# A two-layer hybrid backbone on one core: rows of the Gram tile cleared once per wave on VectorE, rounded row maxima, and a rotation that keeps its own tile

## The chip, the core and the metric

The kernel runs on one core of a Trainium2 chip. The core has five engines that each work through their own list of instructions in a fixed order: TensorE (PE; its weight loads, PEld, are listed apart), VectorE (DVE), ScalarE (ACT), GpSimd (POOL) and SyncE (SP, which here only issues transfers). They wait for each other through semaphores alone. The metric is the time of one execution in microseconds of device time (us), the median of several runs.

## What is computed

Two layers over 256 context tokens and 1024 latent tokens of width 1024. Each layer has one input projection whose columns feed three groups of heads (a bidirectional RWKV-7 recurrence, grouped-query attention with a 2-D rotary rotation, and neighbourhood attention), then one output projection and a layer norm. The parts that the change touches:

```python
def _rwkv7_step(S, inp):                       # 6 heads, both directions, token by token
    r, w, k, v, kk, b = inp
    sa = jnp.einsum('bhvk,bhk->bhv', S, kk)
    S = S * w[:, :, None, :] - sa[..., None] * b[:, :, None, :] + v[..., None] * k[:, :, None, :]
    return S, jnp.einsum('bhvk,bhk->bhv', S, r)

def _apply_axial_rope(x, cos, sin):            # on the latent tokens of q and k of the grouped-query heads
    x1, x2, x3, x4 = jnp.split(x, 4, axis=-1)
    rotated = jnp.concatenate([-x2, x1, -x4, x3], axis=-1)
    return (x * cos[:, None] + rotated * sin[:, None]).astype(x.dtype)

    def one_block(qi):                         # both attentions: a softmax over scores
        s = jnp.einsum('bqgrd,bsgd->bgrqs', qi, keys).astype(jnp.float32)
        p = jax.nn.softmax(s, axis=-1).astype(vals.dtype)
        return jnp.einsum('bgrqs,bsgd->bqgrd', p, vals)
```

## The kernel before

The order of instructions on each engine is set by a scheduler when the program is built; the source order and the dependences are its input. So a small edit can shift the places of many instructions.

**The input projection** (`layer_proj`) multiplies 29 column blocks of 128 with the modulated stream, each product split in three passes of rounded parts (lines 203 to 205, tile `pj`). `qk_proj` handles the keys and the three pairs of query heads of grouped-query attention. It evacuates into `raw` (tile `qr`, two buffers, line 348), normalises it in place, fetches the rotated halves into `rot` by four transfers (line 364), multiplies `rot` by the sine and `raw` by the cosine on POOL (lines 365, 366), adds on DVE into `raw` (line 367) and stores `raw` to DRAM (line 368). The next but one `qk_proj` writes the same buffer of `raw`.

**The recurrence** (`rwkv`) runs in waves of 128 tokens, ten per layer, each with both directions and all six heads; a wave has four chunks of 32 tokens. `wave_pre`, `wave_gram`, `wave_low`, `wave_inv`, `wave_kt` and `wave_merge` prepare a wave two or three waves ahead. `wave_gram` leaves in `G` (six buffers) the masked products of the chunk's vectors. `wave_merge` multiplies blocks of `G` and of the inverse (tile `mg`, line 684): a first round whose result DVE masks into `di` (line 687), and a second round from which DVE makes `tt` (line 689). `wave_chain` then takes the four chunks one after the other: with a tile `X` that stacks, for each direction and head of a pair, the state (64 rows), the values `v` (32 rows, loaded from DRAM at line 706) and the solved rows `sa` (32 rows), it computes `rs` from `G` and `X` (line 713), `sa` from `tt` (line 724, copied into `X` at line 730), the next state `z` (line 734), which DVE scales into the next `X` (line 739), and the output `py` (line 754, in `out_step`, one chunk late). `X` has three buffers. The product for `rs` contracts over all 128 rows, the `sa` rows of the buffer among them, and these still hold what an earlier chunk left there. So POOL sets them to zero in each chunk (line 708, four instructions). The rows of the stacked tile that belong to `sa` are named by `QSA`, those of `v` by `QV`.

**Attention** (`attention`) runs two interleaved generators, woven by the scheduler with the recurrence. `pair_max` computes scores `sm` (line 894) and their row maxima on DVE (lines 896 to 901, tile `nm`, float32). A product with the identity turns each column of 128 maxima into a row, in float32 in the array's column group that begins at 64 (line 907, tile `mt`), and ACT copies it with rounding into row 64 of `q2` (line 908). `pair_main` computes the transposed scores `st` with that row as a 65th term (lines 963, 964), exponentiates (line 970) and multiplies with the values (line 948). Operands of type `F32R` are float32 rounded for a single pass in the array; a float32 product is issued as two instructions.

## Time and profile before

| what | value |
|---|---|
| median of 3 runs | 2448.75 us (2443.36 to 2449.61) |
| the profiled execution, its own time | 2449.5 us |
| its span, first to last instruction | 2447.7 us |
| mean granted TensorE clock | 0.934 of full speed |
| PE busy | 2206.0 us (90% of the span) |
| DVE busy | 1615.7 us (66%) |
| POOL busy | 1180.5 us (48%) |
| ACT busy | 1005.5 us (41%) |
| L907, the products that turn the maxima | 360 instructions, 52.8 us |
| L708, the zeroing of X's rows | 320 instructions, 81.7 us |

A row `L907 PE MATMUL mt<-c_ident,nm` reads: line 907, engine, operation, tile written, tiles read. Busy time of PE counts each product from its start to its modelled end, so overlapping products are counted once and a product's own duration is longer than its distance from the next. "Idle before" and "waits" name the instruction that the profile takes as the one that ended an engine's wait; for a wait on several semaphores it names one of them.

### The profile page before, as it was taken

The page shows a single profiled execution, that of the slowest core. Times are in us where ns is not written, and L with a number is a line of the kernel's source. Part 1 is how long each engine was busy: PE and PEld are TensorE (multiplying, and loading weights), DVE is VectorE, ACT ScalarE, POOL GpSimd, SP SyncE. Part 2 cuts the span into 40 slices and gives each one's busy share as a digit, 9 for nine tenths or more (in the row PEclk, how much of TensorE's full clock was granted, in tenths as well). Part 3 has the DMA queues.
Part 4 walks back from the last instruction along what each step waited for, and adds up shares of the span by engine and source line. Part 5 has one row for each costly group of instructions (what it writes and reads, how often), then busy time and mean ns, then how long its engine had stood idle before and what let it go on. Part 6 is the DMA issues. An engine that isn't in the chain of part 4 may idle for free. (4 is left out here: it accounts for less than half of the span.)

```text
span 2447.7 us, 57800 instructions
## 1 busy us (share of the span) xinstructions
PE 2206.0 (90%) x22616; PEld 1657.5 (68%) x22616; DVE 1615.7 (66%) x3063; ACT 1005.5 (41%) x2186; POOL 1180.5 (48%) x1438
## 2 busy tenths in 40 slices
PE   6999999997887898989999999899969888889897
PEld 3777898775555555555798777697746555556497
DVE  5687434445766878686387797524557788788746
ACT  3333413334544544454343443313345555545522
POOL 3465425424555555454155465533455565565453
PEclk9999999996887999989899999999968999999999
DMA  7344424527445544452233445335464545333342
GB/s 282 111 156 157 134 85 103 144 79 164 111 115 118 122 102 124 125 168 64 73 94 106 136 162 181 112 90 127 113 152 113 117 116 124 81 84 87 100 153 87
DMA packets 448241, 298.17 MB, mean 122 GB/s; under 512 B 249600, under 2 KB 395880, under 8 KB 446944
## 3 DMA queue, kind: packets, MB, share of 16 engines
q1 hardware_dynamic: 439936, 281.71, 41.9%
q0 software_dynamic: 7392, 10.28, 1.6%
q8 instruction: 178, 2.92, 0.5%
q10 hardware_dynamic: 640, 2.49, 0.4%
q14 instruction: 95, 0.78, 0.1%
HBM read 198.37 MB, written 91.79 MB: 119 GB/s over the span
## 5 line engine op out<-in xcount | busy, mean ns | idle before, releaser
L204 PE MATMUL pj<-hlo,wh 128*128 128x512 f32 (+1 forms) x1072 | 402.8, 376 | 13.1 <-DVE hlo L480 7.6
L203 PE MATMUL pj<-hhi,wh 128*128 128x512 f32 (+1 forms) x1072 | 403.2, 378 | 9.2 <-ACT qr L348 5.1
L205 PE MATMUL pj<-hhi,wl 128*128 128x512 f32 (+1 forms) x1072 | 402.0, 376 | 0.2 <-POOL wl L169 0.2
L204 PEld LDWEIGHTS pj<-hlo,wh 128*128 128x128 f32 x1072 | 205.7, 192 | 55.6 <-DVE hlo L480 7.7
L203 PEld LDWEIGHTS pj<-hhi,wh 128*128 128x128 f32 x1072 | 204.8, 192 | 54.3 <-issue 6.8
L169 POOL TENSOR_TENSOR wl<-wf,wh 128x512 fp32r<-128x512 f32 x104 | 142.9, 1379 | 202.7 <-ACT wh L168 185.4
L205 PEld LDWEIGHTS pj<-hhi,wl 128*128 128x128 f32 x1072 | 205.9, 192 | 38.6 <-issue 3.6
L896 DVE TENSOR_REDUCE mx<-sm 128x1 f32<-128x512 f32 (+1 forms) x372 | 199.1, 553 | 46.0 <-PE sm L894 43.7
L948 PE MATMUL y<-pt,v 128*64 128x256 f32 (+1 forms) x1392 | 214.0, 405 | 3.3 <-ACT pt L973 2.4
L970 ACT ACTIVATE pt<-st 128x512 f32<-128x512 f32 (+1 forms) x292 | 163.6, 583 | 129.5 <-PE st L964 125.7
L894 PE MATMUL sm<-k,q 128*128 128x256 f32 (+2 forms) x436 | 167.1, 429 | 34.6 <-DVE mx L896 26.8
L963 PE MATMUL st<-q,k 128*128 128x512 f32 (+3 forms) x376 | 165.9, 445 | 12.5 <-issue 3.5
L1197 PE MATMUL pj<-yl,wh 128*128 128x256 f32 x576 | 165.0, 289 | 2.0 <-POOL yl L1170 2.0
L1196 PE MATMUL pj<-yh,wh 128*128 128x256 f32 x576 | 162.8, 291 | 4.0 <-ACT wh L1147 2.1
L1198 PE MATMUL pj<-yh,wl 128*128 128x256 f32 x576 | 163.2, 288 | 0.1
L977 POOL TENSOR_TENSOR acc<-acc,pt 128x512 f32<-128x512 f32 x80 | 105.4, 1317 | 115.3 <-ACT pt L970 114.4
L948 PEld LDWEIGHTS y<-pt,v 128*64 128x64 f32 x1392 | 94.4, 144 | 90.8 <-issue 60.0
L894 PEld LDWEIGHTS sm<-k,q 128*128 128x128 f32 x436 | 82.8, 208 | 104.6 <-DVE mx L896 42.4
L964 PE MATMUL st<-q,k 65*128 65x512 f32 (+3 forms) x376 | 147.1, 395 | 0.6 <-ACT q L908 0.6
L625 DVE TENSOR_TENSOR G<-gt,msk 64x192 f32<-64x192 f32 (+1 forms) x320 | 110.5, 345 | 43.1 <-PE gt L620 32.0
L708 POOL MEMSET X<- 32x192 f32 x320 | 81.7, 255 | 89.1 <-PE py L754 59.9
L977 DVE TENSOR_TENSOR acc<-acc,pt 128x512 f32<-128x512 f32 x112 | 101.7, 918 | 30.3 <-ACT pt L970 29.8
(276 smaller groups left out, 5113.8 us busy)
## 6 DMA issues: line engine op xcount, KB each, us to landing
wf<-win SPq DMA_DIRECT2D x104, 256.0 KB
wm<-wmod SPq DMA_DIRECT2D x32, 512.0 KB
yf<-yg_d SPq DMA_DIRECT2D x72, 128.0 KB
wt<-wm SPq DMA_DIRECT2D x8, 1024.0 KB
gate_d<-o SPq DMA_DIRECT2D x32, 256.0 KB
wf<-wout SPq DMA_DIRECT2D x16, 512.0 KB
ldkk<-rw_d SPq DMA_DIRECT2D x40, 192.0 KB
ldkd<-rw_d SPq DMA_DIRECT2D x40, 192.0 KB
```

The lines of the kernel that those rows point to most:

```text
L203: nc.tensor.matmul(out=ps[:, :n], lhsT=wh, rhs=hhi[:, k, t0:t0 + n], start=(k == 0), stop=False)
L204: nc.tensor.matmul(out=ps[:, :n], lhsT=wh, rhs=hlo[:, k, t0:t0 + n], start=False, stop=False)
L205: nc.tensor.matmul(out=ps[:, :n], lhsT=wl, rhs=hhi[:, k, t0:t0 + n], start=False, stop=(k == KT - 1))
L894: nc.tensor.matmul(out=sp_[:, :o], lhsT=q[0][:, qc:qc + 128], rhs=k[0][:, c0:c0 + o], start=True, stop=True)
L896: nc.vector.tensor_reduce(out=mx[:, n_:n_ + 1], in_=sp_[:, :o], op=ALU.max, axis=AX.X)
L948: mm = nc.tensor.matmul(out=y[64 * i:64 * i + 64, a0:a1], lhsT=v[:, t, :], rhs=pt[:, p0:p0 + a1 - a0], start=start, stop=stop and at == le ...
L963: nc.tensor.matmul(out=o, lhsT=k[0][:, 128 * t:128 * t + 128], rhs=q[0][:, qa:qb], start=True, stop=False)
L970: nc.scalar.activation(out=pt[:, :w], in_=sp_[:, :w], func=AF.Exp)
L977: eng.tensor_tensor(out=acc[i][:, :w], in0=sums[i][:, :w], in1=pt[:, :w], op=ALU.add)
L1196: nc.tensor.matmul(out=p_, lhsT=wh[m][:, k], rhs=yh, start=(x_ == 0), stop=False)
L1197: nc.tensor.matmul(out=p_, lhsT=wh[m][:, k], rhs=yl, start=False, stop=False)
L1198: nc.tensor.matmul(out=p_, lhsT=wl[m][:, k], rhs=yh, start=False, stop=(x_ == KT - 1))
```

## The change

Three edits. First, in the recurrence, the zeroing of the `sa` rows of `X` in each chunk goes; in its place `wave_merge` sets the `sa` rows of columns 0 to 31 of `G` to zero on DVE, four instructions per wave, once the products of `mg` have read them. All three buffers of `X` are zeroed once at the start of a layer. Second, the maxima are kept rounded in a tile of 72 columns whose first 64 come from the identity; a weight of 65 columns that ends at the wanted one gives the row on partition 64 in one single-pass product over the whole array, with a rounded copy of the identity. Third, `qk_proj` adds into `rot` and stores from there, and the context columns of `raw`, which are not rotated, are stored by a transfer of their own right after the four that fetch the halves.

```diff
--- before.py
+++ after.py
@@ -362,10 +362,12 @@
             rot = sp.tile([128, TL], F32, tag="rot", name="rot")
             for q in range(4):
                 nc.sync.dma_start(out=rot[32 * q:32 * q + 32, :], in_=raw[32 * (q ^ 1):32 * (q ^ 1) + 32, TC:T])
+            if not lo:
+                nc.sync.dma_start(out=dst[:, :TC], in_=raw[:, :TC])
             nc.gpsimd.tensor_tensor(out=rot, in0=rot, in1=sin, op=ALU.mult)
             nc.gpsimd.tensor_tensor(out=raw[:, TC:], in0=raw[:, TC:], in1=cos, op=ALU.mult)
-            nc.vector.tensor_tensor(out=raw[:, TC:], in0=raw[:, TC:], in1=rot, op=ALU.add)
-            nc.sync.dma_start(out=dst[:, lo:], in_=raw[:, lo:])
+            nc.vector.tensor_tensor(out=rot, in0=raw[:, TC:], in1=rot, op=ALU.add)
+            nc.sync.dma_start(out=dst[:, TC:], in_=rot)
 
         def store(dst, b, o):
 
@@ -539,7 +541,8 @@
                 nc.vector.tensor_copy(g[o, :, :, p, :], ident[o, 64 * p:64 * p + 64].unsqueeze(1).unsqueeze(1).to_broadcast([64, 4, 3, 64]))
         NX = 3
         X = [rp.tile([128, 2, 3, 2, 64], F32, tag=f"X{i}", name=f"X{i}") for i in range(NX)]
-        nc.gpsimd.memset(X[0], 0.0)
+        for x in X:
+            nc.gpsimd.memset(x, 0.0)
         lin = rp.tile([128, 16, 16], F32, tag="lin", name="lin")
         nc.gpsimd.memset(lin, 0.0)
 
@@ -687,6 +690,11 @@
                     nc.vector.tensor_tensor(out=po, in0=mg, in1=omk.unsqueeze(1).unsqueeze(1).to_broadcast([128, 4, 3, 32]), op=ALU.mult)
                 else:
                     nc.vector.tensor_tensor(out=tt, in0=mg, in1=di[:, 1], op=ALU.subtract)
+
+            for d in range(2):
+                for p in range(2):
+                    q = QSA[d][p]
+                    nc.vector.memset(gs[d][q:q + 32, :, :, p, 0:32], 0.0)
             prep[w]["tt"] = tt
 
         def wave_chain(w):
@@ -702,10 +710,9 @@
                 for d in range(2):
                     t0 = 128 * wave_block(w, d) + 32 * jc[d]
                     for p in range(2):
-                        q, qs = QV[d][p], QSA[d][p]
+                        q = QV[d][p]
                         nc.sync.dma_start(out=x[q:q + 32, d, :, p, :],
                                           in_=vt_d[t0:t0 + 32, :].rearrange("t (c e v) -> t c e v", c=3, e=2)[:, :, p, :])
-                        ms = nc.gpsimd.memset(x[qs:qs + 32, d, :, p, :], 0.0)
                 for c in range(3):
                     for d in range(2):
                         for p in range(2):
@@ -738,7 +745,7 @@
                         o = slice(64 * p, 64 * p + 64)
                         up = nc.vector.tensor_tensor(out=xn[o, :, :, p, :], in0=z[o], in1=dcj(dc[o, 0, j], j), op=ALU.mult)
                     if j == 1:
-                        mark.update(v=up, g=ms)
+                        mark.update(v=up)
                 if yst is not None:
                     pend.append(lambda j=j, x=x, jc=jc: out_step(w, j, x, jc, gs, yst))
             for f in pend:
@@ -839,6 +846,14 @@
         py = es.enter_context(tc.tile_pool(name=f"py{l}", bufs=1, space=PSUM, side="right"))
         wn = es.enter_context(tc.tile_pool(name=f"wn{l}", bufs=1, **kw))
         ms = mod_spread(((1, 2),) if last else ((0, 2), (1, 1), (1, 0)), wn, pst)
+        identr = ap1.tile([128, 128], F32R, tag="identr", name="identr")
+        nc.vector.tensor_copy(identr, ident)
+
+        nms = [ap1.tile([128, 72], F32R, tag=f"nm{i}", name="nm") for i in range(2)]
+        for z in nms:
+            nc.vector.tensor_copy(z[:, 0:64], ident[:, 0:64])
+            nc.vector.tensor_copy(z[:, 64:72], ident[:, 0:8])
+        nj = [0]
         onec = ap1.tile([128, 32], F32, tag="onec", name="onec")
         nc.vector.memset(onec, 1.0)
 
@@ -882,7 +897,8 @@
 
         def pair_max(q, k, jobs, nq, bias):
 
-            nm = ap2.tile([128, 8], F32, tag="nm", name="nm")
+            nm = nms[nj[0] % 2]
+            nj[0] += 1
             for i, job in enumerate(jobs):
                 q0 = job["q0"]
                 for qt in range(nq // 128):
@@ -898,13 +914,13 @@
                             nc.vector.tensor_tensor_reduce(out=sp_[:, :o], in0=sp_[:, :o], in1=bias[0][:, bcol:bcol + o], scale=1.0, scalar=-3.0e38,
                                                            op0=ALU.add, op1=ALU.max, accum_out=mx[:, n_:n_ + 1])
                         if n_ == len(pcs) - 1:
-                            nc.vector.tensor_reduce(out=nm[:, 4 * i + qt:4 * i + qt + 1], in_=mx[:, :len(pcs)], op=ALU.max, axis=AX.X, negate=True)
+                            nc.vector.tensor_reduce(out=nm[:, 64 + 4 * i + qt:65 + 4 * i + qt], in_=mx[:, :len(pcs)], op=ALU.max, axis=AX.X, negate=True)
                         yield
             for i, job in enumerate(jobs):
                 q0 = job["q0"]
                 mt = pst.tile([128, 512], F32, tag="sm", name="mt", bufs=2)
                 for qt in range(nq // 128):
-                    nc.tensor.matmul(out=mt[64:65, 128 * qt:128 * qt + 128], lhsT=nm[:, 4 * i + qt:4 * i + qt + 1], rhs=ident, start=True, stop=True, tile_position=(0, 64))
+                    nc.tensor.matmul(out=mt[0:65, 128 * qt:128 * qt + 128], lhsT=nm[:, 4 * i + qt:4 * i + qt + 65], rhs=identr, start=True, stop=True)
                 nc.scalar.copy(q[1][64:65, q0:q0 + nq], mt[64:65, :nq])
                 yield
```

The order differs in many places; three are shown. The first is on DVE, where the merge of the fourth wave of the first layer stands, before (`acc`, `pt`, `mx`, `sm`, `nm`: attention; `yo`: the recurrence's output; `lin`, `nn`: the inverse of the next wave):

```order
L982 TENSOR_TENSOR acc_10158<-acc_10158,pt_10233 128x384
L687 TENSOR_TENSOR di<-mg,omk 128x384
L901 TENSOR_REDUCE nm<-mx 128x1
L972 TENSOR_TENSOR pt_10247<-st,bt 128x384
L972 TENSOR_TENSOR pt_10254<-st,bt 128x384
L792 TENSOR_REDUCE sm<-yo 128x6
L898 ISA sm,mx<-sm,bs 128x384
L898 ISA mx 128x1
L896 TENSOR_REDUCE mx<-sm 128x1
L645 COPY nn<-lin 64x256
L793 TENSOR_SCALAR sm<-sm 128x6
```

The same place on DVE after the change (line 690 is the former 687, line 912 the former 896, line 647 the former 644):

```order
L647 COPY nn<-lin 64x256
L998 TENSOR_TENSOR acc_10050<-acc_10050,pt_10124 128x384
L697 MEMSET G_2952 32x12x32 x2
L690 TENSOR_TENSOR di<-mg,omk 128x384
L697 MEMSET G_2953 32x12x32 x2
L988 TENSOR_TENSOR pt_10145<-st,bt 128x384
L917 TENSOR_REDUCE nm<-mx 128x1
L797 TENSOR_TENSOR yo<-yo,sm 128x384
L914 ISA sm,mx<-sm,bs 128x384
L914 ISA mx 128x1
```

Two of the four new instructions stand ahead of the mask that the second round of `mg` waits for, and two behind it, ahead of `tt`.

The second place is POOL, at the preparation of a later wave of the first layer (`G`, `lp`, `kb`: the wave's tiles; `acc`: attention's sums), before:

```order
L593 MEMSET G_2950 64x12x64 x2
L593 MEMSET G_2951 64x12x64
L708 MEMSET X_2967 32x3x64 x3
L593 MEMSET G_2951 64x12x64
L708 MEMSET X_2967 32x3x64
L570 DMA zs<-zs_d 98x128
L977 TENSOR_TENSOR acc_11072<-pt_11077,pt_11096 128x512
L570 DMA zs<-zs_d 98x128
L594 TENSOR_TENSOR G_2950<-ldkk,lp 64x3x4x32
L596 TENSOR_TENSOR G_2950<-ldr,lp 64x3x4x32
```

POOL after the change, at the same preparation (line 596 is the former 593):

```order
L596 MEMSET G_2954 64x12x64 x2
L596 MEMSET G_2955 64x12x64 x2
L998 TENSOR_TENSOR acc_10958<-acc_10958,pt_11063 128x384
L573 DMA zs<-zs_d 98x128
L998 TENSOR_TENSOR acc_10958<-acc_10958,pt_11081 128x256
L998 TENSOR_TENSOR acc_10959<-acc_10959,pt_11081 128x128
L890 TENSOR_TENSOR q_11282<-stg,q_11282 64x1280
L573 DMA zs<-zs_d 98x128
L1058 TENSOR_TENSOR ys<-ys,gtl 128x512
L597 TENSOR_TENSOR G_2954<-ldkk,lp 64x3x4x32
L599 TENSOR_TENSOR G_2954<-ldr,lp 64x3x4x32
```

What is gone are the zeroings of `X` between the others. No other engine takes over POOL's work; the four instructions per wave on DVE are all that is added there in the recurrence.

The third place is PE at the first wave of the first layer, where before the products for `rs` stood early, ahead of that wave's `mg` (line 684):

```order
L713 MATMUL ch<-X_2966,G_2949 32x64
L635 MATMUL kt<-c_ident,kb 128x128 x3
L713 MATMUL ch<-X_2966,G_2949 32x64
L713 MATMUL ch<-X_2966,G_2948 32x64 x2
L713 MATMUL ch<-X_2966,G_2949 32x64 x2
L713 MATMUL ch<-X_2966,G_2948 32x64 x2
L713 MATMUL ch<-X_2966,G_2949 32x64 x2
```

After the change they stand behind the `mg` products (line 687), which read what is then cleared:

```order
L720 MATMUL ch<-X_2970,G_2952 32x64
L203 MATMUL pj<-hhi,wh 128x512
L720 MATMUL ch<-X_2970,G_2952 32x64
L204 MATMUL pj<-hlo,wh 128x512
L687 MATMUL mg<-di 32x32 x48
L638 MATMUL kt<-c_ident,kb 128x128 x3
L720 MATMUL ch<-X_2970,G_2953 32x64 x2
L720 MATMUL ch<-X_2970,G_2952 32x64 x2
L720 MATMUL ch<-X_2970,G_2953 32x64 x2
L720 MATMUL ch<-X_2970,G_2952 32x64 x2
L720 MATMUL ch<-X_2970,G_2953 32x64 x2
```

They moved some 250 rows down PE's list, to where the products with `tt` follow.

## Rows read from the trace of the kernel before

**Rows 1.** The page: busy time and share of the span of each engine, the granted TensorE clock in 40 slices, and the shares by engine of the chain of work that ended last.

```profile
PE 2206.0 (90%) x22616; PEld 1657.5 (68%) x22616; DVE 1615.7 (66%) x3063; ACT 1005.5 (41%) x2186; POOL 1180.5 (48%) x1438
PEclk9999999996887999989899999999968999999999
PE 23%; DVE 12%; DMA 5%; ACT 3%; issue 3%; POOL 2%; SPq 1%; DVEq 0%; ACTq 0%; POOLq 0%
```

**Rows 2.** The chain in order of time: its first piece (start, length, engine, tile and line), which tells how far back it reaches.

```profile
1246.37 1.14 DVE sq L154 x2
```

**Rows 3.** Busy time by stretch: length, then PE, PEld, DVE, ACT and POOL busy with the count of instructions, granted clock, share of the DMA engines, GB/s. The first four rows cover the time of the chain in quarters; the last two are the stretches in which recurrence and attention run together, in the first and in the second layer.

```profile
1200.00:1500.00 300.00, 288.21 (x1704) 251.35 (x1704) 233.18 (x223) 112.53 (x188) 154.84 (x175) 0.97 0.39 126
1500.00:1800.00 300.00, 278.94 (x2137) 226.81 (x2137) 136.70 (x245) 98.28 (x218) 130.78 (x156) 0.96 0.48 132
1800.00:2100.00 300.00, 255.05 (x4007) 169.14 (x4005) 240.00 (x634) 146.98 (x357) 170.59 (x234) 0.91 0.51 117
2100.00:2448.00 348.00, 309.74 (x3654) 228.47 (x3649) 246.90 (x440) 151.70 (x328) 164.77 (x198) 0.96 0.34 98
...
571.00:1063.00 492.00, 428.05 (x6512) 282.09 (x6511) 365.07 (x944) 239.86 (x602) 253.50 (x351) 0.86 0.48 115
...
1804.00:2290.00 486.00, 429.07 (x6648) 278.08 (x6647) 395.64 (x966) 245.07 (x587) 268.26 (x357) 0.94 0.43 102
```

**Rows 4.** PE in order of time (start, length, line, operation, tiles, shape, count): twice the products that turn the maxima, between the neighbours.

```profile
607.99 0.39 PE L894 MATMUL sm<-k,q 128*128 128x256 f32 x1
608.30 1.03 PE L907 MATMUL mt<-c_ident,nm 128*1 128x128 f32 x8
609.26 0.54 PE L724 MATMUL ch<-rsb,tt 32*32 32x64 f32 x24
609.73 0.81 PE L907 MATMUL mt<-c_ident,nm 128*1 128x128 f32 x6
```

**Rows 5.** One line's instructions, L907: its weight loads and its products (count, least, median and most ns of one).

```profile
L907 PEld LDWEIGHTS mt<-c_ident,nm x360: 79/84/128, 574.8 to 2293.1; 128*1 128x1 f32 x180
L907 PE MATMUL mt<-c_ident,nm x360: 270/272/421, 574.8 to 2293.2; 128*1 128x128 f32 x180
```

**Rows 6.** PE in order of time: products of rounded operands with 128 columns, one behind the other.

```profile
985.86 0.28 PE L964 MATMUL st<-q,k 65*128 65x128 f32 x1
985.97 0.28 PE L963 MATMUL st<-q,k 128*128 128x128 f32 x1
986.08 0.28 PE L964 MATMUL st<-q,k 65*128 65x128 f32 x1
```

**Rows 7.** The longest pieces of the chain that are L907 (start, length, count).

```profile
1838.19 3.50 PE mt L907 x16
...
2010.74 1.62 PE mt L907 x14
...
2199.44 1.62 PE mt L907 x14
...
2247.84 1.62 PE mt L907 x14
...
2291.59 1.92 PE mt L907 x16
```

**Rows 8.** One line's instructions, zeroings on DVE of other sizes: L260 with 1280 elements in each partition, L1189 with 128 (least, median and most ns).

```profile
L260 DVE MEMSET stg<- x4: 1125/1125/1125, 61.2 to 1352.4; 2x1280 f32 x4
```

```profile
L1189 DVE MEMSET ones<- x2: 165/165/165, 1198.7 to 2327.5; 128x128 f32 x2
```

**Rows 9.** Waits of PE, and one of its weight loads, by what ended them: us in total, times, longest.

```profile
PE sm L894 <- DVE mx L896: 26.8, 23, 3.4
PE py L754 <- DVE tt L689: 14.4, 9, 3.4
...
PE ch L713 <- DMA X<-vt_d: 8.7, 4, 4.4
PE ch L713 <- POOL X L708: 8.6, 5, 3.0
...
PE kt L635 <- DVE tt L689: 5.1, 4, 2.2
```

```profile
PEld ch L713 <- POOL X L708: 17.1, 11, 4.5
```

**Rows 10.** Groups by line, with shapes kept apart: busy us and mean ns, then the idle time before them and what ended it. The zeroing of X on POOL.

```profile
L708 POOL MEMSET X<- 32x192 f32 x320 | 81.7, 255 | 89.1 <-PE py L754 59.9 <-PE ch L734 11.7 <-PE ch L713 2.0
```

**Rows 11.** The longest single wait that the profile puts down to POOL's zeroing, about 1930 us: PE, then POOL, then DVE, in order of time.

```profile
1932.64 1.27 PE L713 MATMUL ch<-X,G 128*32 128x64 f32 x24 [2.97 <-POOL X L708]
```

```profile
1928.57 3.65 POOL L708 MEMSET X<- 32x192 f32 x12
```

```profile
1931.42 1.12 DVE L739 TENSOR_TENSOR X<-ch,dc 64x384 f32<-64x384 f32 x2
```

**Rows 12.** The rotation in the second layer, about 1565 us: pieces of the chain, then ACT and PE in order of time.

```profile
1564.86 2.30 DVE qr L367
1567.17 3.04 DMA k_d<-qr
```

```profile
1570.45 0.69 ACT L348 ACTIVATE qr<-pj,pp 128x512 f32<-128x512 f32 x1 [9.78 <-DMA k_d<-qr]
```

```profile
1571.19 0.80 PE L203 MATMUL pj<-hhi,wh 128*128 128x512 f32 x1 [4.78 <-ACT qr L348]
```

## The prediction

> **What bounds the kernel now.** I read the page first. PE is busy for 90% of the span, DVE for 66%, POOL for 48% [rows 1]: PE is nearest to being the bound, but a product on PE counts as busy while it only waits for its own end, so this alone says little. Next I looked at the chain of work that ended last. It is traced back from the end to 1246 us [rows 2], and of the whole span PE has 23%, DVE 12% and POOL 2% on it [rows 1]. Set against what the engines are busy in the same time [rows 3], that says how much of an engine's work ends up in the time. PE: 0.23 x 2447.7 = 563 us of 288.21 + 278.94 + 255.05 + 309.74 = 1132, a share of 0.50. DVE: 294 of 857, 0.34. POOL: 49 of 621, 0.08. No engine is the bound by itself; half of what PE does counts, a third of what DVE does, and hardly anything of what POOL does. The change touches the two stretches where recurrence and attention run together: there PE is busy for 428 of 492 us and 429 of 486, DVE for 365 (0.74) and 396 (0.81), POOL for 254 (0.52) and 268 (0.55) [rows 3]. The chain's first half is not shown, so I take these shares, found in the later part, for both layers. They are an estimate; each term below gets ends of its own.
>
> **The turned maxima.** There are 180 float32 products, each issued as two: 360 instructions [rows 5]. Six that begin at 609.73 take 0.81 us in all, and one takes 0.272, so they follow each other every (0.81 - 0.27) / 5 = 0.108 us [rows 4, 5]; 360 x 0.108 = 38.9 us of PE. Afterwards there are 180 single-pass products, also of 128 columns. The nearest rows are the scores of 128 columns with rounded operands, which follow each other every 0.11 us, each with its own weights of 128 columns [rows 6]: 180 x 0.11 = 19.8 us. So 19.1 us of PE go. For a lower price there is no row; if the 65-column weights halve it, 29 us go. The share on the path: the chain's five longest pieces of this line hold 16 + 14 + 14 + 14 + 16 = 74 of the second layer's 160 instructions [rows 7], 0.46, close to the 0.50 above. I take 0.50: **-9.5 us**, ends 0 (PE waits for DVE instead, as it does at the scores for 26.8 us [rows 9]) and -29.
>
> The products also change their place in the array. Before, eight of them begin at 608.30 and the next, of another shape, at 609.26: 0.96 us where 8 x 0.108 = 0.86 would do, so the change of shape takes 0.10 [rows 4]. TensorEngine Tiling in the Trainium skill says (Key Properties) that changing the tiling mode, not merely the tile, drains the array. By that rule, which this row bears out, the new whole-array products save the drain beside scores, which use the whole array too, and pay it beside the recurrence's column products, where the old ones paid none. There are 60 groups with two ends each, so at worst 120 x 0.10 x 0.50 = 6.0 us come back. I take nothing for it, since both kinds of neighbour occur, and put the worst with the no-change rival.
>
> **The clearing on DVE.** Each new instruction clears 12 x 32 = 384 elements in each of 32 partitions. Zeroings on DVE of 1280 and of 128 elements take 1125 and 165 ns [rows 8], so one more element costs 0.833 ns and 384 of them 165 + 256 x 0.833 = 378 ns. Four in each of 20 waves: 80 x 0.378 = 30.2 us. With DVE's share of 0.34 this is **+10.3 us**. A second way to the same size: PE stands waiting for `tt` 9 + 4 = 13 times [rows 9], and the order puts two clearings ahead of the mask that the second round of `mg` needs, which delays `tt` by 2 x 0.378 = 0.76 us, while the other two run beside the second round; 13 x 0.76 = 9.9 us. Queued behind the clearings on DVE are `di`, `tt`, the row maxima (PE waits for those longest) and the state update of line 739. Ends: 0, if they fall into DVE's own gaps, and +30.2, if every one delays the chain.
>
> **The zeroing that goes.** POOL loses 320 instructions and 81.7 us [rows 10]. The waits view puts 8.6 us of PE's waiting for `rs` down to it [rows 9], but its largest case is not what it seems: the products start at 1932.64, POOL's twelve zeroings end at 1932.22 (four of them are this chunk's), and the state update on DVE ends at 1932.54, 0.1 us before [rows 11]. So `rs` was waiting for the state all the same. The transfer of `v` into the same buffer stays, with its wait for an earlier `py`, and it ended 8.7 us of PE's waits itself [rows 9]. Directly I therefore count nothing. Indirectly, POOL's later work (the scaled rows of `G`, the parts of q and k, attention's sums) no longer queues behind these instructions, nor behind their 59.9 us of waiting for `py` [rows 10]. By POOL's share of 0.08 that is **-6.5 us**; ends 0 and -26 (third rival).
>
> **The rotation.** Only once does ACT wait for the buffer of `raw`: 9.78 us, up to 1570.45, which holds up PE for 4.78 [rows 12]. What it waits for at the end is the store, 3.04 us from its issue, after the addition on DVE that ends at 1567.17. Afterwards the addition is the last reader and the store reads `rot`, so the wait ends some 3 us earlier: **-3.0 us**, on the chain as a whole [rows 12]; ends 0 and -4.8. The store now holds `rot`, whose next writer but one comes two projections later. The added store of the context columns, five in all, is issued while POOL multiplies. Clearing all three X at the start, and the copies that set up the identity, are a few instructions per layer beside the projection: nothing. At a layer's first wave `rs` now stands behind `mg`, but so did the product with `tt` that needs it: nothing, up to +2.
>
> **Sum.** -9.5 + 10.3 - 6.5 - 3.0 = -8.7 us against the profiled execution's 2449.5: 2440.8. That execution lies 0.75 above the median, so for the median I say 2440. Since the scheduler also moves many instructions by some places, this is good to about 7 us: 2433 to 2447.
>
> **The rivals.**
>
> *DVE becomes the bound.* At 0.81 busy in the second layer's stretch [rows 3] it has little room, and all 30.2 us could land on the path, with POOL's relief worth nothing: 30.2 - 9.5 - 3.0 = +17.7, so 2466. From a share of (9.5 + 3.0) / 30.2 = 0.41 on the kernel is slower than before, which isn't far above the 0.34 taken. Against it: DVE still waits for PE and ACT in these stretches, a fifth to a quarter of the time. Chance 0.20.
>
> *Nothing is left.* The clearings fit into DVE's gaps, PE's relief turns into longer waits for DVE at the scores or is paid back in changes of shape, POOL's relief hides: only the 3.0 of the rotation stays, 2446. Chance 0.16.
>
> *POOL counted after all.* PE and its weight loads wait for the zeroing as the views say; with 8.6 on the one and 17.1 on the other [rows 9], which overlap, 17.1 more go: -8.7 - 17.1 = -25.8, 2423. Speaking against it is the case in [rows 11]. Chance 0.14.
>
> *The products aren't cheaper.* Loading 65 weight columns instead of one could make a single product as slow as the two were; the loads took 84 ns each [rows 5]. Then -6.5 - 3.0 + 10.3 = +0.8, 2449.5. Against it are the 0.11 us with 128 weight columns [rows 6]. Chance 0.05.
>
> **Chances and range.** A measurement of this kernel can tell about 0.3% from no change, 7.3 us: faster is below 2441.4, slower above 2456.1. The forecast has 0.45, of which 0.29 lies below 2441.4 and 0.16 above. Faster: 0.29 + 0.14 = 0.43. Same: 0.16 + 0.16 + 0.05 = 0.37. Slower: 0.20. The range runs from the third rival's 2422 to 2461, the nearer half of the first rival; what lies beyond has some 0.2.
>
> **What would show it.** L907's successor should have 180 products, a fifth of a microsecond to a tenth apart, and fewer pieces on the chain. The clearings should be 80 DVE rows of about 378 ns, and the wait of `py` and `kt` for `tt` should grow by up to 10 us; if it grows by 20 or if DVE is above 0.85 busy in the second layer's stretch, the first rival is right. `rs` should go on starting about 0.1 us behind the state update: if it starts earlier than in the rows of before and the chunks come closer together, the third is. ACT's 9.78 us wait at the rotation should shrink to about 6.7. I am wrong altogether if the granted clock of a stretch moves by some hundredths, or if the new order on PE lets attention and recurrence hinder each other in another way.

## The result and the profile after

The changed kernel takes 2422.95 us (median of 4 runs, 2420.58 to 2430.1) where the kernel before takes 2446.06 beside it (4 runs, 2440.74 to 2449.61): a ratio of 0.9904, 95% interval 0.9877 to 0.9931, some 23 us less. The forecast was 8.7 us less. The profiled execution took 2430.1 us, with a span of 2428.3.

The page after, the rows that answer to [rows 1]:

```profile
PE 2172.0 (89%) x22436; PEld 1635.1 (67%) x22436; DVE 1647.0 (68%) x3153; ACT 1005.9 (41%) x2186; POOL 1105.4 (46%) x1122
PEclk9999999996898989999999999999888889999899
PE 51%; DVE 21%; DMA 11%; ACT 5%; issue 5%; SPq 3%; POOL 2%; DVEq 0%; ACTq 0%; POOLq 0%
```

PE is busy for 34 us less, DVE for 31 more, POOL for 75 less; the last two are near what the counts gave (30.2 more, and 81.7 less with 2.7 for the four added zeroings of whole tiles `X`; POOL's busy time differs by 4 us between two executions of the kernel before). The two profiled executions are 19 us apart in span, so PE's idle time grew by 15 us, from 242 (248 in a second execution, e12) to 256. This alone doesn't say where 23 us went. The chain reaches back through the whole span here.

The pieces that were forecast one by one. First the turned maxima (one line's instructions, then PE in order of time around eight of them), to be held against [rows 4, 5]:

```profile
L923 PEld LDWEIGHTS mt<-identr,nm x180: 133/137/235, 573.0 to 2263.4; 128*65 128x65 f32 x180
L923 PE MATMUL mt<-identr,nm x180: 218/226/455, 573.1 to 2263.5; 128*65 128x128 f32 x180
```

```profile
2046.38 0.65 PE L923 MATMUL mt<-identr,nm 128*65 128x128 f32 x8
2046.87 0.44 PE L979 MATMUL st<-q,k 128*128 128x512 f32 x1
```

Eight products take 0.65 us and one 0.226, so they follow each other every (0.65 - 0.226) / 7 = 0.061 us, where 0.11 was taken. The clearings on DVE, then waits of PE (us, times, longest), to be held against [rows 9]:

```profile
L697 DVE MEMSET G<- x80: 378/378/378, 449.1 to 2195.5; 32x384 f32 x80
```

```profile
PE ch L720 <- DVE X L746: 19.9, 13, 3.8
PE sm L910 <- DVE mx L912: 18.3, 20, 5.2
...
PE py L761 <- DVE tt L692: 12.1, 5, 6.1
...
PE mt L923 <- DVE nm L917: 10.8, 5, 4.5
PE ch L720 <- DMA X<-vt_d: 10.1, 3, 5.1
...
PE kt L638 <- DVE tt L692: 0.2, 1, 0.2
```

The waits for `tt` did not grow. What ended the idle time before the products for `rs` (weight loads and products together), first in the kernel before, then after:

```profile
POOL X L708: 25.6, 16
...
DVE X L739: 14.3, 18
DMA X<-vt_d: 8.7, 4
```

```profile
DVE X L746: 45.1, 31
...
DMA X<-vt_d: 13.1, 7
```

POOL is gone from the list, and the state update took its place: 25.6 + 14.3 + 8.7 = 48.6 us before, 45.1 + 13.1 = 58.2 after. The rotation's evacuation on ACT in the second layer (what ended its idle time, who waited for it), against [rows 12]:

```profile
DVE rot L369: 10.3, 2
...
PE pj L203: 2.0, 1
```

```profile
1534.79 1.27 ACT L348 ACTIVATE qr<-pj,pp 128x512 f32<-128x512 f32 x2 [7.03 <-DVE rot L369]
1535.53 0.50 PE L203 MATMUL pj<-hhi,wh 128*128 128x512 f32 x1 [2.03 <-ACT qr L348]
```

ACT's longest wait there went from 9.78 to 7.03 us (6.7 was expected, and there is a second one of 3.3), PE's from 4.78 to 2.03.

Where the time went is seen by stage, a stage being bounded by the recurrence's first and last `z`, attention's last `y` and the projection's first and last `pj`. Between the last `z` and the last `y` of a layer attention runs alone: its **tail**. Below, the kernel before has its second execution (e12) beside the first; lengths in us, with the granted clock:

| stage | before | before, again | after |
|---|---|---|---|
| up to layer 1's first `z` | 470 / 0.98 | 475 / 0.97 | 471 / 0.98 |
| layer 1, recurrence with attention | 592 / 0.87 | 589 / 0.88 | 585 / 0.90 |
| layer 1, attention's tail | 132 / 0.90 | 131 / 0.91 | 102 / 0.95 |
| output projection | 125 / 0.97 | 124 / 0.99 | 124 / 0.99 |
| layer 2, input projection | 457 / 0.97 | 452 / 0.98 | 451 / 0.98 |
| layer 2, recurrence with attention | 506 / 0.92 | 513 / 0.91 | 529 / 0.89 |
| layer 2, attention's tail | 35 / 1.00 | 35 / 1.00 | 29 / 0.94 |
| the rest | 131 / 0.93 | 128 / 0.93 | 137 / 0.90 |

The tails gave 36 us, the second layer's recurrence took some 20 back. Of the operations that the change touches, a tail holds only products that turn maxima: in the two tails together they keep PE busy for 9.9 us before and 3.5 after, partly because fewer of them are left there. For the rest a tail is shorter because less of attention is left in it. Busy time of the line of `y` alone in the two tails (length, then PE with its count and PEld with its count; each product is two instructions), before and after:

```profile
1062.42:1194.31 131.89, 38.08 (x255) 17.35 (x256) 0.90 0.34 102
2281.91:2316.75 34.84, 14.13 (x103) 6.63 (x104) 1.00 0.32 88
```

```profile
1056.20:1158.10 101.90, 31.70 (x224) 14.67 (x224) 0.95 0.36 114
2261.78:2290.59 28.81, 10.95 (x80) 4.95 (x80) 0.94 0.34 94
```

Of the value products, 256 / 2 = 128 and 52 stood behind the last `z` before; 112 and 40 do after. That is in the order of the instructions on PE, which the scheduler made when the program was built.

### The profile page after: what moved, and what is told of

It is laid out like the page before. It is cut to its first block, busy times and chain, and to the rows that moved or that the text cites. A ratio compares the mean times of both kernels' runs of the same rounds, so it can differ in the third digit from the quotient of the medians.

```text
span 2428.3 us, 56945 instructions
## 1 busy us (share of the span) xinstructions
PE 2172.0 (89%) x22436; PEld 1635.1 (67%) x22436; DVE 1647.0 (68%) x3153; ACT 1005.9 (41%) x2186; POOL 1105.4 (46%) x1122
## 4 chain that ended last, share of the span: by engine, by line
PE 51%; DVE 21%; DMA 11%; ACT 5%; issue 5%; SPq 3%; POOL 2%; DVEq 0%; ACTq 0%; POOLq 0%
PE pj L204 5%; PE pj L205 5%; PE pj L203 5%; PE y L964 4%; PE st L979 3%; PE sm L910 2%; PE pj L1212 2%; PE pj L1214 2%; DMA ls_d<-G 2%; PE pj L1213 2%; DVE G L628 2%; DVE mx L912 2%; PE st L980 2%; DVE tmp L656 2%; DMA lin<-ls_d 2%
## 5 line engine op out<-in xcount | busy, mean ns | idle before, releaser
L910 PE MATMUL sm<-k,q 128*128 128x256 f32 (+2 forms) x436 | 173.2, 432 | 25.6 <-DVE mx L912 18.3
L168 ACT CAST wh<-wf 128x512 fp32r<-128x512 f32 x104 | 64.1, 621 | 136.6 <-DMA wf<-win 89.4
L1212 PEld LDWEIGHTS pj<-yh,wh 128*128 128x128 f32 x576 | 110.8, 195 | 12.8 <-ACT yh L1185 7.9
```

Source lines behind the costliest of these rows:

```text
L910: nc.tensor.matmul(out=sp_[:, :o], lhsT=q[0][:, qc:qc + 128], rhs=k[0][:, c0:c0 + o], start=True, stop=True)
L1212: nc.tensor.matmul(out=p_, lhsT=wh[m][:, k], rhs=yh, start=(x_ == 0), stop=False)
```

## The experiments

Three theories. **Theory 1**: the forecast's terms hold one by one. **Theory 2**: it is work taken away that gives the time, but a term was mis-sized (2a: the clearings cost nothing; 2b: POOL's zeroing held up `rs` as the views say). **Theory 3**: the order decides, whatever the work. Each kernel is timed against the kernel before on the same chip, and profiled. The expectations name layers as the first and the second; a "ratio" is of times. Of each edit only the lines that matter are printed; an interval in parentheses is one of 95%.

**e1, the maxima alone**, on the kernel before:

```diff
-                    nc.tensor.matmul(out=mt[64:65, ...], lhsT=nm[:, 4 * i + qt:4 * i + qt + 1], rhs=ident, ..., tile_position=(0, 64))
+                    nc.tensor.matmul(out=mt[0:65, ...], lhsT=nm[:, 4 * i + qt:4 * i + qt + 65], rhs=identr, ...)
```

> The kernel before with only the rounded maxima. Theory 1 (the forecast's terms hold one by one, and the surplus comes from the terms of the recurrence): 9.5 us less, ratio 0.996. Theory 2 (the turned maxima are what was mis-sized, PE's 19 us count in full): 19 us less or more, ratio 0.992 or below. Theory 3 (the new order of instructions decides, not the work): some value between -15 and +15 us that the work removed does not explain, and the three edits alone will not add up to the whole.

Measured: ratio 0.9954 (0.9931 to 0.9977), -11 us. That is theory 1's number, and theory 3 allows it too.

**e2, the recurrence's edit alone**:

```diff
-                        ms = nc.gpsimd.memset(x[qs:qs + 32, d, :, p, :], 0.0)
+                    nc.vector.memset(gs[d][q:q + 32, :, :, p, 0:32], 0.0)
```

> The kernel before with only the recurrence's edit: rows of G cleared on VectorE, X's rows no longer zeroed. Theory 1: +10.3 - 6.5 = +3.8 us, ratio 1.0016. Theory 2a (VectorE's clearings fall into its gaps, POOL's relief is all that is left): -6.5 us, ratio 0.997. Theory 2b (the views were right that the products for rs wait for POOL): -6.5 - 17.1 = -24 us, ratio 0.990, which would be the whole gain of the change. Theory 3: between -15 and +15 us, with no relation to either term.

Measured: ratio 1.0042 (1.0022 to 1.0062), +10 us. Alone, this edit makes the kernel slower; of 2a's -6.5 and 2b's -24 us nothing is seen. But its tails are 10 us longer than before, with as many products behind the last `z` (in a profiled execution of 2475.15 us, the longest of twelve), and the runs with an edit to the order alone, below, move the kernel by more than 10 us, so this run by itself doesn't rule 2a and 2b out.

**e3, the rotation alone**:

```diff
-            nc.vector.tensor_tensor(out=raw[:, TC:], in0=raw[:, TC:], in1=rot, op=ALU.add)
-            nc.sync.dma_start(out=dst[:, lo:], in_=raw[:, lo:])
+            nc.vector.tensor_tensor(out=rot, in0=raw[:, TC:], in1=rot, op=ALU.add)
+            nc.sync.dma_start(out=dst[:, TC:], in_=rot)
```

> The kernel before with only the rotation's own tile. Theory 1: 3.0 us less, ratio 0.999, from the wait of ScalarE in the second layer's projection. The rival that the projection gained more (its stretch was some 6 us shorter after the whole change): 6 us less, ratio 0.9975. Theory 3: between -15 and +15 us, with gains or losses in stretches in which no rotation runs.

Measured: ratio 0.9919 (0.9891 to 0.9948), -20 us, from an edit that can save 5 us of PE's waiting, and more than any of the three theories had expected (theory 3 stopped at 15). Its first layer's tail is 119 us, with 240 instructions of `y` (120 products):

```profile
1059.44:1178.81 119.37, 34.44 (x240) 15.79 (x240) 0.91 0.35 105
```

**e4, the change without the recurrence's edit** (e1 and e3 together).

> The changed kernel without the recurrence's edit: maxima and rotation alone, X's rows zeroed on POOL as before. Theory 1: -9.5 - 3.0 = -12.5 us, ratio 0.995. Theory 2b (the recurrence's edit carries the gain): near -5 us or less, ratio 0.998. If the recurrence's edit brings nothing in the whole: -23 us, ratio 0.990. Theory 3: not the sum of the two edits alone within 8 us.

Measured: ratio 0.9924 (0.9897 to 0.9951), -19 us; e1 and e3 would add to -31. The effects of the edits don't add, as theory 3 has it. The three alone do add to -21, near the whole's -23, but by accident, as this run and the next ones show.

**e5 and e6, the rotation in one layer only**:

```diff
-            nc.sync.dma_start(out=dst[:, lo:], in_=raw[:, lo:])
+            if l == 1:        # e5; l == 0 in e6
+                nc.vector.tensor_tensor(out=rot, in0=raw[:, TC:], in1=rot, op=ALU.add)
+                nc.sync.dma_start(out=dst[:, TC:], in_=rot)
```

> The kernel before with the rotation's edit in the second layer only. There stands the one wait that the edit was forecast to shorten; in the first layer the order of every engine stays exactly as before, and in the second layer the attention's products stand some 20 to 80 places earlier on TensorE. Theory 1 (the rotation saves what e3 showed, as work): about -20 us, ratio 0.992, since the first layer's rotation never waited. Theory 3 (order): the first layer's tail of attention after the recurrence stays at 132 us instead of e3's 120, the projection gives the 3 us of the wait, and the whole is -3 to -8 us, ratio 0.997 to 0.999.

> The kernel before with the rotation's edit in the first layer only, where no engine was seen to wait for it. The order of the first layer is that of e3 (the attention's products up to 200 places earlier than before on TensorE); that of the second layer has the attention's products up to 200 places later. Theory 1: 0 us, ratio 1.000. Theory 3: the first layer's tail at 120 us as in e3, -12 us, and a longer tail in the second layer (35 us before), by some 10 us: about 0 in all, with both parts visible.

Measured: e5 1.0007 (0.9979 to 1.0036), e6 1.0033 (1.001 to 1.0056). In the layer where the wait stood, the rotation's edit shortens it (PE's wait there is 1.6 us) and the total doesn't move by an amount that can be told (-5 to +9 us, where theory 1 put -20 and theory 3 -3 to -8). In e6 the first layer's tail is e3's, and the second layer's has grown to 75 us with 79 products, where theory 3 put some 45:

```profile
1064.95:1184.40 119.45, 34.54 (x239) 15.81 (x240) 0.91 0.34 105
2276.94:2351.91 74.97, 23.62 (x157) 10.69 (x158) 0.94 0.37 114
```

So e3's 20 us are not what the rotation's work gives by itself in either layer.

**e7 and e8, the order alone**: the kernel before with no part of the change, and an instruction or three more on POOL that nothing waits for.

```diff
+        if l == 0:                                    # e7, where X is set up
+            for i in range(3):
+                nc.gpsimd.memset(X[0], 0.0)
```

```diff
+        if l == 0:                                    # e8, where attention is set up
+            pad = ap1.tile([128, 128], F32, tag="pad", name="pad")
+            nc.gpsimd.memset(pad, 0.0)
```

> The kernel before with no part of the change: three more zeroings of one tile on GpSimd at the start of the first layer's recurrence, beside the projection. They shift the order: the first layer's attention products stand up to 280 places earlier on TensorE than before (up to 240 in the changed kernel), the second layer's some 60 places earlier at first and later at the end. Theories 1 and 2 (the work that the change removes gives the time): no gain, ratio 1.000 to 1.001. Theory 3 (order): the first layer's tail shrinks from 132 to 100 to 120 us, and the whole is 10 to 25 us shorter, ratio 0.990 to 0.996.

> The kernel before with no part of the change: one zeroing of 128 columns on GpSimd when the first layer's attention is set up. It shifts the order: the first layer's attention products stand up to 240 places earlier on TensorE, the second layer's up to 100 places later. Theories 1 and 2: no change, ratio 1.000. Theory 3: the first layer's tail near 120 us, -12 us, and some 5 us back in the second layer: -7 us, ratio 0.997.

Measured: e7 0.9925 (0.9899 to 0.995), -18 us; e8 1.0119 (1.0085 to 1.0153), +29 us. Work was added in both, and one is faster by as much as most of the change, the other slower by more. The tails, e7 and then e8:

```profile
1068.94:1168.68 99.74, 29.15 (x191) 13.31 (x192) 0.90 0.38 113
2256.66:2312.10 55.44, 19.13 (x127) 8.40 (x128) 0.97 0.39 118
```

```profile
1087.25:1206.67 119.42, 35.70 (x239) 16.14 (x240) 0.90 0.35 105
2297.71:2365.20 67.49, 21.84 (x144) 9.55 (x144) 0.97 0.43 129
```

The sign of e8 was expected wrongly: its second layer's tail is 67 us, not 40, and the first layer's recurrence took 613 us instead of 592. The tail follows the order; that stretch's 21 us more are not explained by any count made here. e8 also adds a small tile, which e7 does not; whether that matters beside the order was not separated.

**e9, the change's work in a later order**: the changed kernel with one more zeroing of that kind, chosen because it leaves 128 and 52 products behind the last `z`, as before.

```diff
+        for i in range((1, 0)[l]):
+            nc.gpsimd.memset(X[0], 0.0)
```

> The changed kernel whole, with one more zeroing of a tile on GpSimd at the start of the first layer's recurrence. It shifts the order so that, as in the kernel before, 128 and 52 of attention's value products (y) stand behind the recurrence's last z in the two layers, where the changed kernel has 112 and 40. The work is that of the change. Theories 1 and 2 (the gain is the work taken away): 2423 us, ratio 0.990. Theory 3 (the gain is the order): the tails come out near 132 and 35 us as before, and what is left is the work's own price, 0 to -10 us, ratio 0.996 to 1.000.

Measured: ratio 0.997 (0.995 to 0.9991), -7 us; theory 3's number, and 16 us away from the changed kernel, whose interval doesn't touch this one. The tails:

```profile
1066.22:1195.96 129.74, 38.32 (x255) 17.43 (x256) 0.88 0.33 102
2268.80:2303.45 34.65, 13.91 (x103) 6.71 (x104) 1.00 0.32 85
```

**e10, an order meant to be better still**: e4 with three such zeroings in the first layer.

> The kernel of e4 (maxima and rotation, X's rows zeroed on GpSimd as before) with three more zeroings of a tile on GpSimd at the start of the first layer's recurrence, which leave 104 and 52 value products behind the last z, where e4 has 116 and 52. Theories 1 and 2: as e4, 2428 us, ratio 0.992. Theory 3: the first layer's tail at 105 to 110 us instead of 120, and 2415 us, ratio 0.987, the shortest of all.

Measured: ratio 0.9905 (0.9874 to 0.9935), -23 us. The first layer's tail is 107 us, as expected, and the total no better than the changed kernel's; against e4's 0.9924 the intervals overlap, and theory 3's 0.987 lies outside this one. A version that beats both kernels was not found.

**e11, the clearings twice**:

```diff
                     nc.vector.memset(gs[d][q:q + 32, :, :, p, 0:32], 0.0)
+                    nc.vector.memset(gs[d][q:q + 32, :, :, p, 0:32], 0.0)
```

> The changed kernel with every clearing on VectorE issued twice: 80 x 378 ns = 30.2 us more on that engine; the order leaves 116 and 40 value products behind the last z, close to the 112 and 40 of the changed kernel. The forecast's term (a third of VectorE's time counts): +10.3 us over the changed kernel, 2433 us, ratio 0.9945. The clearings fall into gaps: as the changed kernel but for 4 us of tail, 2427 us or less, ratio 0.992. All of it counts: +30 us, 2453 us, ratio 1.003.

Measured: ratio 1.003 (1.0009 to 1.0052), +7 us over the kernel before, so some 31 over the changed kernel (0.0126 x 2446): the number for "all of it counts". Its tails, 116 and 34 us, are 14 + 5 = 19 longer than the changed kernel's, which leaves some 12; against e9, whose tails are 15 us longer than e11's, it is 15 us slower, so there all 30 count. PE's wait for `tt` in the output is longer than the changed kernel's 12.1 us, but hardly longer than in the second profile of the kernel before (e12), which clears nothing on DVE. First e11, then e12:

```profile
PE py L762 <- DVE tt L692: 20.4, 8, 7.1
```

```profile
PE py L754 <- DVE tt L689: 18.8, 8, 4.0
```

Nor is PE idle for longer in all: 257 us for the changed kernel's 256 in the profiled executions. It is busy for 24 us more, with the same count of instructions (2196.4 us for 2172.0), at a granted clock of 0.912 for 0.935. So that the clearings fall into gaps and cost nothing is unlikely, but the trace doesn't show the 30 us as waits for them; how much is DVE's time, how much the clock and how much the order stays open.

**e12, the kernel before again**, for its profile.

> The kernel before once more, for a second profile: how much the lengths and granted clocks of its stages differ from one execution to the next. If the tails are set by the order, they come out as in the first profile within 3 us (132 and 35); stretches that the clock sets may differ by 10 us or more, the second layer's recurrence (506 us at 0.92) above all.

Its time was 2449.04 us. The tails came out at 131 and 35 us, with the same 128 and 52 products; the second layer's recurrence at 513 us with clock 0.91, its projection at 452 instead of 457. So a tail is the same from run to run, while the 6 us by which the changed kernel's projection seemed shorter are, but for 1 us, what two executions of one kernel differ.

```profile
1063.79:1195.24 131.45, 38.40 (x255) 17.53 (x256) 0.91 0.34 102
2283.87:2318.71 34.84, 14.13 (x103) 6.63 (x104) 1.00 0.33 88
```

Its chain reaches through the whole span, and puts 0.49 x 2447.3 = 1199 us of PE's 2199.8 busy ones on the path, 0.55, DVE's share at 0.30 of 1620.5 and POOL's at 0.08 of 1176.5: the shares that the forecast took from the later half were not the mistake.

```profile
PE 49%; DVE 20%; DMA 13%; issue 6%; ACT 5%; POOL 4%; SPq 3%; DVEq 0%; POOLq 0%; ACTq 0%
```

All kernels in one table; "behind" is the count of value products behind the last `z` in the first and second layer, "change" is (ratio - 1) x 2446 us, and "clock" is the granted clock, the mean over the kernel's timed executions:

| kernel | work | behind | tails, us | change, us | clock |
|---|---|---|---|---|---|
| before | before | 128, 52 | 132, 35 | 0 | 0.934 |
| e7 | before | 96, 64 | 100, 55 | -18 | 0.939 |
| e8 | before | 120, 72 | 119, 67 | +29 | 0.929 |
| e1 | maxima | 124, 40 | 121, 30 | -11 | 0.928 |
| e2 | clearing | 128, 52 | 136, 41 | +10 | 0.933 |
| e3 | rotation | 120, 52 | 119, 35 | -20 | 0.939 |
| e5 | rotation, layer 2 | 128, 52 | 132, 35 | +2 | 0.929 |
| e6 | rotation, layer 1 | 120, 79 | 119, 75 | +8 | 0.933 |
| e4 | maxima, rotation | 116, 52 | 120, 35 | -19 | 0.927 |
| e10 | maxima, rotation | 104, 52 | 107, 34 | -23 | 0.929 |
| e9 | all | 128, 52 | 130, 35 | -7 | 0.927 |
| after | all | 112, 40 | 102, 29 | -23 | 0.933 |
| e11 | all, clearing twice | 116, 40 | 116, 34 | +7 | 0.920 |

The tail goes with the count: 0.91 to 1.06 us for each product in the first layer, 0.67 to 0.95 in the second. The changed kernel's own first tail is the one furthest off, 102 us for 112 products (clock 0.95) where e11's takes 116 for 116 (clock 0.88), so the count doesn't explain all of the 36 us. And the tail does not set the total alone: e6 and e8 have tails of like sum and differ by 21 us.

The last column adds something that the counts don't hold. The six kernels with the turned maxima have a clock of 0.920 to 0.933, the seven others 0.929 to 0.939. Three of them give PE the same products: the changed kernel, e9 and e11. From one to the next the time rises (2423, 2438 and 2456 us) and the clock falls (0.933, 0.927, 0.920). The pages of e9 and then e11, to be held against the changed kernel's 2172.0:

```profile
PE 2185.5 (90%) x22436; PEld 1646.0 (68%) x22436; DVE 1650.0 (68%) x3153; ACT 1005.6 (41%) x2186; POOL 1104.4 (45%) x1123
```

```profile
PE 2196.4 (90%) x22436; PEld 1657.4 (68%) x22436; DVE 1678.8 (68%) x3233; ACT 1005.5 (41%) x2186; POOL 1107.5 (45%) x1122
```

With spans of 2428.3, 2434.0 and 2453.6 us, PE is idle for 256, 249 and 257 us: the changed kernel has the least busy time of the three, by 13 and 24 us, at the highest clock, and not the least idle time. So what it gains over the other two stands in PE's busy time, not in shorter waits. Whether the order moves the clock, and by what, is not shown; e8 and e10 have the same 0.929 and lie 52 us apart, so the clock isn't the whole of it either.

## Why the prediction was right, and where its size was off

**Direction and range held; the size was off by some 15 us, and the step that failed is the last one of the sum**: "Since the scheduler also moves many instructions by some places, this is good to about 7 us". With no part of the change, edits to the order alone moved the kernel by -18 and +29 us (e7, e8). The narrow range, 2433 to 2447, missed by 10 us. The wide one held by 1 us, and its end at 2422 was the third rival's number, whose mechanism wasn't borne out (below): that it held is luck.

With as many products behind the last `z` as before, the changed kernel measures -7 us (e9, -12 to -2), near the -8.7 of the sum. That doesn't prove the sum: the count doesn't fix the total (e6 and e8), and its terms may have been off in opposite directions, as told below. What is shown is that the same work, but for one zeroing of 0.7 us on POOL, is 16 us apart in two orders. In the changed kernel's order the two tails are 36 us shorter; the second layer's recurrence gives some 20 us back, at a clock of 0.89 for 0.92 and 0.91. Why that stretch is longer is open: in the kernels with other edits and orders it is 509 to 535 us. The prediction's own sign of being wrong, a clock that moves by some hundredths in a stretch, came true there and in the first tail (0.95 for 0.90 and 0.91).

**The turned maxima.** The spacing was mis-sized: 0.061 us instead of 0.11, so PE saves 38.9 - 180 x 0.061 = 27.9 us, not 19.1. The scores with 128 weight columns [rows 6] were the wrong neighbour; the lower end, "if the 65-column weights halve it", was the right one. Half of 27.9 is 14; e1 measured -11 in an order of its own (tails 16 us shorter), so the share that counts isn't settled by it. Part of the relief turned into a new wait, PE for `nm`, 10.8 us, while the scores' wait for `mx` went from 26.8 to 18.3. On the changes of shape: the score product behind the eight at 2046.38 starts at 2046.87, 0.06 us after the last of them began. TensorEngine Tiling (Array Packing) in the Trainium skill (Key Properties) has the array drained when the tiling mode changes; both use the whole array, and the trace agrees that nothing is lost between them. What the column products' neighbours pay was not measured by itself.

**Clearing and zeroing.** Duration and count were exact, 80 x 378 ns. The pair was forecast at +3.8 and measured +10 alone (e2, +5 to +15). The share of DVE's time that was taken, 0.34, lies below what e11's times leave (0.4 to 1), so this term may have been too small; e11 doesn't separate it from the clock and the order. Its second way to that size fails: the wait for `tt` didn't grow in the changed kernel (12.1 us in the output for [rows 9]'s 14.4, and 0.2 for 5.1 at `kt`).

**POOL's zeroing.** The reading that `rs` waited for the state all the same is borne out: the idle time once put down to POOL stands under the state update now. The rival by which POOL counted gave 2423, the time that was measured, for a reason that the runs don't bear out: without any of POOL's relief the kernel has 19 of the 23 us, in an order of its own (e4). A matching number is no evidence for its mechanism.

**The rotation.** The wait was read rightly and fell by 2.8 us on PE; nothing of it can be told in the total (e5). The stage shows more than the total does: the second layer's projection takes 440 to 451 us in the seven profiles with the edit in that layer and 447 to 457 in the seven without it, 7 us less on average, so this term may have been too small.

**The other rivals.** DVE did not become the bound: 415.91 of 528.78 us in the second layer's recurrence, 0.79. The products got cheaper, and something was left.

```profile
1733.00:2261.78 528.78, 446.48 (x6795) 290.05 (x6794) 415.91 (x1029) 257.01 (x616) 250.46 (x243) 0.89 0.45 104
```

**What could have been read beforehand.** The order of both kernels was there. Counting the `y` products behind the last `z`, 128 and 52 against 112 and 40, with 131.89 / 128 = 1.03 and 34.84 / 52 = 0.67 us each, would have given -16 and -8 us as a term of its own, with a wide range; the tails measured -30 and -6. The places that were shown instead are where the edits sit, not where the order decides.

## What to carry to other kernels

Where two streams of work are woven by a scheduler, count first what the new order leaves of the one when the other ends, and price that by the length of the lonely tail; a small edit far away can move it more than its own work is worth. Before a gain of a per cent is credited to an edit, time the old kernel with an idle instruction or two added: here that alone gave -18 and +29 us. And hold busy time, idle time and granted clock of the bounding engine apart: here kernels with the same products differed by up to 24 us in PE's busy time, at another clock. Single edits measured one by one don't add up in such a kernel, and a sum that fits may be an accident.

## What the runs showed of the hardware that was not expected

Rounded products of 128 columns, each with its own weights, followed each other every 0.061 us with 65 weight columns (at 2046.38) and every 0.11 with 128 [rows 6], both in stretches where the clock was granted in full (1.00, 2.4 GHz). The latter also alternate between 128 and 65 rows; that the weight columns alone set the distance was not tried by itself.

Executions of one kernel differ, and mostly the longer ones have the lower granted clock: among 23 runs of the kernel before on one chip the shortest took 2424.18 us at a mean clock of 0.941 and the longest 2460.19 at 0.928. That is 36 us, more than the whole change; only the number of runs makes a difference of 0.4% visible. The clock isn't all of it: among 23 runs on another chip the shortest (2438.11 us) and the longest (2458.5) both had 0.931.
